# The high parts of the weight blocks by a converting DMA instead of a ScalarE cast

## The chip, the cores and the metric

One core of a Trainium2 chip runs the whole program. The metric is the device time of one execution in microseconds (us).

## The reference

The program is one step of a two-layer decoder trunk, D = 1024, on 1024 prompt tokens and 8 x 4 sample tokens that carry their own states. Cut to what the matmuls see:

```python
# layer 0, Hawk: W_LRU = 1536
xn = rmsnorm(x, g0)
xb, gate = split(xn @ a_w_in)            # 1024 -> 2 x 1536
h = rg_lru(causal_conv(xb))              # gates from 16 blocks of 96 x 96, then a scan over time
x = x + (h * silu(gate)) @ a_w_out       # 1536 -> 1024
# layer 1, HGRN2: 8 heads of 128
xn = rmsnorm(x, g1)
q, f, v, gate = split(xn @ b_w_in)       # 1024 -> 4 x 1024
o = gated_linear_recurrence(silu(q), f, v)
x = x + (rmsnorm(o) * silu(gate)) @ b_w_out
y = rmsnorm(x, final_gain)
```

The outputs are y and the new states, all in float32.

## The kernel before

Channels lie on the 128 partitions and tokens along the free axis. There are 1024 + 32 = 1056 columns, cut into three chunks of 352 (`CH`). The host has laid the weights out by output tile of 128 channels, so that one tile's weights are one 128 x 1024 matrix (an *item*): two blocks of 128 x 512, four K steps of 128 in each.

Products keep float32 accuracy with three matmuls in the shorter float32r type. A value x is held as a high part, x rounded to float32r, and a low part, x minus that. `mm3` (L239 to L243) multiplies high by high (L241), high weight by low activation (L242), low weight by high activation (L243). One item on one chunk is 8 K steps or 24 matmuls; on all three chunks it is 72.

The function `weights` (L371) prepares the blocks of one item. For each block SP issues a DMA of the float32 values from DRAM to a buffer `raw`; ScalarE (ACT) casts it to the high part (L383); then `subtract` (L313) gives the low part as raw minus high, on GpSimd (POOL) in the default case `e is G`, on VectorE (DVE) where the caller asks for it. `get` then hands out the K steps. The buffers go round in rings: three of `raw` (`wraw` in the profile), four of the high part (`whi`), four of the low part (`wlo`). With `at` the high and low parts go to places that the caller names, and the rings of high and low are left alone.

Those who call `weights`:

- `begin` (L862): the first six items of layer 0, in the first 60 us. Four of them split on DVE, and four have places of their own.
- `project0` (L414) and `by_chunk` (L421): the other input projections of layer 0, the gates and the convolution inputs.
- `out` (L634): output rows of layer 0, blocks of 128 x 384.
- `first1` (L715) and the dictionary `ahead` behind it: the first items of layer 1.
- the loop over `wo1` (L1629): output rows of layer 1, five K steps each, so a block of 512 and one of 128; the first two rows have places of their own.

Two other places prepare weights without it: `out_last` casts the last 384 K rows of layer 0's output weights by itself, and layer 1's head products (`seven`) use `low` (L315), where ACT writes minus the high part and POOL issues a DMA that adds the raw value to it in SBUF.

The order of the work is not written out by hand. Each operation of layer 0 goes into a list (class `Flow`) with its engine, an assumed duration, the keys that it reads and writes, and a priority. `plan` schedules the list on five queues (PE, DVE, ACT, POOL, SP) with a simple model of the DMA engines; `back` does the same from the end, to give each operation a latest start as its new priority; eight rounds of both are run, the best is kept, and `search` then tries 3000 random shifts of the operations planned in the first 60 us. The engines get their instructions in the resulting order. Layer 1 is a second list without the search. So a changed duration or engine of one kind of operation can move others anywhere in its layer.

PE runs this sequence of products in layer 0: the first six items chunk by chunk (`products`), gate(1), conv(1), gate(2), conv(2), out(0), gate(3) in part, conv(3), out(1), the rest of gate(3), `out_last`, `first1`. 48 filling matmuls of `ones` (L734) keep PE busy until data is there. Before `out_last`, `norm` and `scaled_parts` (L463) make the normalised activations that the next layer multiplies. In `first1` ACT takes a tanh of the product (L724) and POOL makes the two gate rows ST and a from it (L726), of which layer 1's first decay factors are made.

Of the kernel before, what the change touches and what calls it, by code (L numbers as in the profile page):

```python
# [209 lines left out]
def tile_trunk(ctx: ExitStack, tc: tile.TileContext, xT, prm, hc, w0, wg, wo0, w1, wo1, s_in,  # L210
               yT, h_out, c_out, sp_out, ss_out):
    nc = tc.nc
    V, S, G, T, Q = nc.vector, nc.scalar, nc.gpsimd, nc.tensor, nc.sync
# [82 lines left out]
    with ExitStack() as l0:  # L296
        pl = l0.enter_context(tc.tile_pool(name="l0", bufs=1, reuse_waits="tile"))
        fl = Flow("PE")

        def fixed(name, shape, dt=F32, pool=None):  # L300
            return (pool or pl).tile(shape, dt, tag=name, name=name)
# [7 lines left out]
        def dma(dst, src, r=(), w=(), prio=5, kb=180, q=Q):  # L309
            fl.add("SP" if q is Q else "ACT", 0.45, lambda: q.dma_start(dst, src), r, w, prio, kb * (1.0 if r else 0.75))  # L310
# [6 lines left out]
        def act(n, emit, r, w, prio=5, more=0.0):  # L317
            fl.add("ACT", 0.25 + 0.0007 * n + more, emit, r, w, prio)
# [7 lines left out]
        def subtract(e, n, b, x, a, r, w, prio):  # L326

            emit = lambda: e.tensor_tensor(b, x, a.bitcast(F32), op=ALU.subtract)  # L328
            if e is G:
                pool(n, emit, r, w, prio)  # L330
            else:
                dve(n, emit, r, w, prio, True)
# [38 lines left out]
        def weights(src, n, prio=2, e=G, at=None, q=Q, own=()):  # L371

            own = iter(own)
            got = []
            for a in range(0, n, 512):
                m = min(512, n - a)
                raw, *rk = next(own, None) or next(raws)
                if at:
                    (hi, hk), (lo, lk) = ((o[:, a:a + m], k) for o, k in at)
                else:  # L380
                    (hi, hk), (lo, lk) = next(his), next(los)
                dma(raw[:, :m], src[:, a:a + m], (), rk, prio, m / 2, q)
                act(m, lambda hi=hi, raw=raw, m=m: S.copy(hi[:, :m], raw[:, :m]), rk, (hk,), prio)  # L383
                subtract(e, m, lo[:, :m], raw[:, :m], hi[:, :m], (*rk, hk), (lk,), prio)
                got.append((hi, lo, hk, lk))

            def get(k):
                q = slice((k % 4) * 128, (k % 4 + 1) * 128)
                hi, lo, hk, lk = got[k // 4]
                return hi[:, q], lo[:, q], (hk, lk)  # L390

            return get
# [18 lines left out]
        def project0(items):  # L411

            for src, evac in items:
                w = weights(src, 1024)  # L414
                for c in range(NCH):
                    evac(c, *product(w, xcols(c)))
                    yield

        def by_chunk(items):

            ws = [weights(src, 1024) for src, _ in items]  # L421
            for c in range(NCH):
                for w, (_, evac) in zip(ws, items):
                    evac(c, *product(w, xcols(c)))
                    yield
# [204 lines left out]
        def out(g, src, dst):  # L630

            own = cycle([next(xos) for _ in range(NXO)] + [next(ts) for _ in range(3)] + [(x[:, :CH], k) for x, k in (next(xbs) for _ in range(3))])
            for m in range(KD):
                w = weights(wo0[m][:, 384 * g:384 * g + 384], 384)  # L634
                for c in range(NCH):
                    ps, pk = product(w, ycols(c))
                    x, xk = next(own)
                    dma(x, src[m][:, chunk(c)], ((g, m, c),), (xk,), 3)
                    dve(CH, lambda x=x, ps=ps: V.tensor_tensor(x, ps[:, :CH], x, op=ALU.add), (pk, xk), (xk,), 0)
                    dma(dst[m][:, chunk(c)], x, (xk,), ((g + 1, m, c),), 3)  # L640
                    yield
# [208 lines left out]
        raw = (halves[1][:8], [slots[i] for i in (1, 4, 7, 2, 5, 8)] + [halves[1][8], free[8]], free[:8])  # L850
# [82 lines left out]
    with ExitStack() as l1:  # L933
        p1 = l1.enter_context(tc.tile_pool(name="l1", bufs=1, reuse_waits="tile"))
        fl = Flow(side=0.4)
# [7 lines left out]
        at = fixed("attn", [128, 8, 128], F32, p1)  # L943
# [702 lines left out]
        for m in range(KD):  # L1646
            row = (xh, xl)[m // 4][4 + m % 4]
            hi, lo, hk, lk = row[:, :nl], row[:, nl:2 * nl], ("late", m, 0), ("late", m, 1)
            for k in (hk, lk):
                inherit(k, [("x", p, m % 4, x) for p in (2, 3) for x in range(2)])  # L1650
            raw, rk = next(raws)
# [60 lines left out]
        for a, n in OUT:  # L1712
# [4 lines left out]
            for m in range(KD):  # L1717
# [5 lines left out]
                hi, lo, wk = late[m]  # L1723
# [97 lines left out]
```

## Time and profile before

| | us |
|---|---|
| median of 2 runs | 1075.01 (1074.71 to 1075.32) |
| the profiled execution | 1074.84 |
| its span in the profile | 1073.1 |
| PE busy | 1050.9 |
| DVE busy | 745.6 |
| ACT busy | 663.7 |
| POOL busy | 504.5 |

The span runs from the first to the last recorded event; 1.74 us of the execution's time lie outside it. PE is TensorE's matmuls and PEld its weight loads, which overlap them; SP only issues DMAs. L383 is line 383 of the code. In a group of instructions stand line, engine, operation, output <- input, shape and count; behind the first bar the busy time and the mean duration in ns of one; behind the second the engine's idle time just before them and what ended most of it. A row of the timeline has start, duration, engine, line, operation and, in square brackets, the idle time before it with what ended it. A row on a releaser (`PE mm L242 <- POOL xl L328: 0.7, 1, 0.7`) has the total wait, how often, and the longest. Lines of DMA issues have the count, the size of one and the median time from issue to landing in us; the transfer lines that begin with q0 have packets, megabytes and the share of sixteen DMA engines over the span.

### The profile page before, as it was taken

The page shows a single profiled execution, that of the slowest core. Times are in us where ns is not written, and L with a number is a line of the kernel's source. Part 1 is how long each engine was busy: PE and PEld are TensorE (multiplying, and loading weights), DVE is VectorE, ACT ScalarE, POOL GpSimd, SP SyncE. Part 2 cuts the span into 40 slices and gives each one's busy share as a digit, 9 for nine tenths or more (in the row PEclk, how much of TensorE's full clock was granted, in tenths as well). Part 3 has the DMA queues.
Part 4 walks back from the last instruction along what each step waited for, and adds up shares of the span by engine and source line. Part 5 has one row for each costly group of instructions (what it writes and reads, how often), then busy time and mean ns, then how long its engine had stood idle before and what let it go on. Part 6 is the DMA issues. An engine that isn't in the chain of part 4 may idle for free.

```text
span 1073.1 us, 25672 instructions
## 1 busy us (share of the span) xinstructions
PE 1050.9 (98%) x10020; PEld 1023.3 (95%) x10020; DVE 745.6 (69%) x1481; ACT 663.7 (62%) x1493; POOL 504.5 (47%) x536
## 2 busy tenths in 40 slices
PE   9999999999999999999989999999999999999997
PEld 9999999999999999999989998989999999989996
DVE  7999996887987787274887556556565475674446
ACT  6578656867765964243467685858586767652323
POOL 3425353354543547455454454455455464541544
PEclk9999999999999999999989999999999999999999
DMA  9111112124832785373675564746465657555204
GB/s 302 60 28 43 56 48 72 58 60 127 270 104 67 217 258 168 108 242 121 188 200 110 130 140 100 178 93 156 89 151 112 155 112 169 140 161 166 84 1 162
DMA packets 92490, 139.59 MB, mean 130 GB/s; under 512 B 11344, under 2 KB 60496, under 8 KB 92368
## 3 DMA queue, kind: packets, MB, share of 16 engines
q1 hardware_dynamic: 75952, 109.49, 31.8%
q0 software_dynamic: 14112, 25.70, 14.3%
q10 hardware_dynamic: 2304, 2.77, 0.8%
q8 instruction: 78, 1.28, 0.5%
q14 instruction: 44, 0.36, 0.1%
HBM read 77.54 MB, written 29.81 MB: 100 GB/s over the span
## 4 chain that ended last, share of the span: by engine, by line
PE 86%; DVE 9%; DMA 3%; issue 1%; ACT 1%; POOL 0%; POOLq 0%; ACTq 0%; SPq 0%; DVEq 0%
PE mm L241 24%; PE mm L242 24%; PE mm L243 23%; PE hg L1057 2%; PE hg L1166 2%; DMA a<-xn 1%; PE hg L1274 1%; PE hg L572 1%; DVE R L1039 1%; PE hg L1276 1%; PE hg L241 1%; PE hg L242 1%; PE hg L243 1%; PE hg L1220 1%; DVE a L1240 1%
## 5 line engine op out<-in xcount | busy, mean ns | idle before, releaser
L241 PE MATMUL mm<-xh,whi 128*128 128x352 f32 (+1 forms) x1111 | 346.6, 312 | 5.7 <-DVE sg L1510 5.7
L242 PE MATMUL mm<-xl,whi 128*128 128x352 f32 (+1 forms) x1111 | 340.7, 307 | 0.0
L243 PE MATMUL mm<-xh,wlo 128*128 128x352 f32 (+1 forms) x1111 | 340.6, 307 | 0.0
L241 PEld LDWEIGHTS mm<-xh,whi 128*128 128x128 f32 x1111 | 209.0, 188 | 8.3 <-DVE sg L1510 6.8
L242 PEld LDWEIGHTS mm<-xl,whi 128*128 128x128 f32 x1111 | 209.3, 188 | 1.5
L243 PEld LDWEIGHTS mm<-xh,wlo 128*128 128x128 f32 x1111 | 209.1, 188 | 0.0
L328 POOL TENSOR_TENSOR wlo<-wraw,whi 128x512 fp32r<-128x512 f32 (+1 forms) x72 | 96.3, 1347 | 105.7 <-ACT whi L383 97.2
L241 PE MATMUL mm<-t,whi 128*128 128x264 f32 (+1 forms) x354 | 104.0, 294 | 0.0
L243 PE MATMUL mm<-t,wlo 128*128 128x264 f32 (+1 forms) x354 | 101.8, 288 | 2.0 <-DMA wlo<-wraw 2.0
L242 PE MATMUL mm<-t,whi 128*128 128x264 f32 (+1 forms) x354 | 101.9, 288 | 0.0
L504 DVE SCALAR_TENSOR_TENSOR k<-xb,prm_sb,k 128x352 f32<-128x352 f32 (+2 forms) x144 | 90.0, 636 | 11.0 <-ACT k L501 6.3
L315 POOL DMA_DIRECT2D wlo<-wraw x59 | 51.6, 888 | 65.6 <-ACT wlo L314 46.6
L1510 DVE TENSOR_TENSOR k<-mm,k 128x264 f32<-128x264 f32 x72 | 30.7, 430 | 62.2 <-PE mm L243 59.4
L243 PEld LDWEIGHTS mm<-t,wlo 128*128 128x128 f32 x354 | 67.2, 190 | 2.3 <-DMA wlo<-wraw 2.3
L241 PEld LDWEIGHTS mm<-t,whi 128*128 128x128 f32 x354 | 67.5, 191 | 0.5 <-ACT k L1487 0.2
L242 PEld LDWEIGHTS mm<-t,whi 128*128 128x128 f32 x354 | 67.5, 191 | 0.0
L587 POOL TENSOR_TENSOR k<-X 128x352 f32<-128x352 f32 x36 | 42.8, 1198 | 47.8 <-DVE R L588 38.6
L383 ACT CAST whi<-wraw 128x512 fp32r<-128x512 f32 (+2 forms) x75 | 41.3, 569 | 31.3 <-PE mm L242 19.8
L315 POOL DMA_DIRECT2D wlo<-R x36 | 33.5, 929 | 49.7 <-ACT wlo L314 48.2
L241 PE MATMUL mm<-yh,whi 128*128 128x352 f32 x153 | 49.9, 326 | 0.0
L243 PE MATMUL mm<-yh,wlo 128*128 128x352 f32 x153 | 49.4, 323 | 0.0
L242 PE MATMUL mm<-yl,whi 128*128 128x352 f32 x153 | 49.4, 323 | 0.0
(422 smaller groups left out, 2742.1 us busy)
## 6 DMA issues: line engine op xcount, KB each, us to landing
wraw<-in_w_dram SPq DMA_DIRECT2D x88, 256.0 KB, 3.1
wlo<-wraw POOLq DMA_DIRECT2D x59, 256.0 KB, 4.1
wlo<-R POOLq DMA_DIRECT2D x36, 256.0 KB, 4.0
wraw<-in_wo_dram SPq DMA_DIRECT2D x34, 192.0 KB, 2.5
si<-in_s_in_dram SPq DMA_DIRECT2D x8, 512.0 KB, 4.5
R<-in_w_dram SPq DMA_DIRECT2D x16, 256.0 KB, 3.8
out_ss_out_dram<-si SPq DMA_DIRECT2D x8, 512.0 KB, 2.6
sg<-x1b SPq DMA_DIRECT2D x21, 176.0 KB, 3.1
```

The costliest lines, as they stand in the source:

```text
L241: T.matmul(out, wh, xh, start=first, stop=False, skip_group_check=chained)
L242: T.matmul(out, wh, xl, start=False, stop=False, skip_group_check=chained)
L243: T.matmul(out, wl, xh, start=False, stop=last, skip_group_check=chained)
L315: fl.add("POOL", 0.93, lambda: G.dma_start(dst.bitcast(F32), src, accum_op=ALU.add), (*r, *w), w, prio, n / 2)
L328: emit = lambda: e.tensor_tensor(b, x, a.bitcast(F32), op=ALU.subtract)
L383: act(m, lambda hi=hi, raw=raw, m=m: S.copy(hi[:, :m], raw[:, :m]), rk, (hk,), prio)
L504: dve(u, lambda src=src, dst=dst, sh=sh, k=k: V.scalar_tensor_tensor(dst, sh(src, k), pc("cw", 12 * k + m), dst, op0=ALU.mult, op1=ALU.add ...
L572: fl.add("PE", 0.62, lambda ps=ps, i=i, c=c: T.matmul(ps[:96, :CH], gs[:, i, :], ST[:96, chunk(c)], start=True, stop=True), (("gs",), *((" ...
L587: pool(CH, lambda x=x, a=a, b=b: G.tensor_tensor(x, a.bitcast(F32), b.bitcast(F32), op=ALU.add), (ak, bk), (xk,), 3)
L1057: T.matmul(ps[32 * j:32 * j + 32, n * w:n * w + w], B[:, o:o + 32], q(slice(o, o + 32)), start=True, stop=True, tile_position=(0, 32 * j))
L1166: T.transpose(ps[:, n * 128:(n + 1) * 128], row[:, a:a + 128], ident)
L1510: dve(QT, lambda: V.tensor_tensor(o[0], z[0], u[0], op=ALU.add), (z[1], u[1]), (o[1],), 0)
```

## The change

Where `weights` splits on POOL and no places are named, the high part no longer comes from `raw`. POOL issues a second DMA of the same block from DRAM, into the float32r buffer, and the conversion is left to the DMA. The raw block is still loaded by SP, and the subtraction on POOL is as before; it now follows two transfers. The other blocks keep the cast.

```diff
@@ -380,7 +380,10 @@
                 else:
                     (hi, hk), (lo, lk) = next(his), next(los)
                 dma(raw[:, :m], src[:, a:a + m], (), rk, prio, m / 2, q)
-                act(m, lambda hi=hi, raw=raw, m=m: S.copy(hi[:, :m], raw[:, :m]), rk, (hk,), prio)
+                if e is G and at is None:
+                    fl.add("POOL", 0.95, lambda hi=hi, m=m, a=a: G.dma_start(hi[:, :m], src[:, a:a + m]), (), (hk,), prio, m / 2)
+                else:
+                    act(m, lambda hi=hi, raw=raw, m=m: S.copy(hi[:, :m], raw[:, :m]), rk, (hk,), prio)
                 subtract(e, m, lo[:, :m], raw[:, :m], hi[:, :m], (*rk, hk), (lk,), prio)
                 got.append((hi, lo, hk, lk))
```

72 blocks take the new way: 44 of 128 x 512 of the input projections (36 in layer 0, 8 in layer 1), 16 of 128 x 384 in `out`, and 12 of the layer-1 output rows (six of 512, six of 128). Three casts stay. Lines behind L382 are three higher in the changed kernel; the new DMA is L384.

Layer 1's order is nearly the same but for the replaced instructions. Layer 0 is planned anew. Three places of it follow; `x3` behind a row means three such in a row.

PE, start of the program. `hg<-ones` are the filling matmuls, `whi` and `wlo` the parts of the first item's weights, `xh` and `xl` those of the activations. Before:

```order
L734 MATMUL hg<-ones 128x128 x29
L241 MATMUL mm<-xh,whi 128x352
L242 MATMUL mm<-xl,whi 128x352
L243 MATMUL mm<-xh,wlo 128x352
L241 MATMUL mm<-xh,whi 128x352
L242 MATMUL mm<-xl,whi 128x352
L243 MATMUL mm<-xh,wlo 128x352
L734 MATMUL hg<-ones 128x128 x9
L241 MATMUL mm<-xh,whi 128x352
L242 MATMUL mm<-xl,whi 128x352
L243 MATMUL mm<-xh,wlo 128x352
L734 MATMUL hg<-ones 128x128 x2
```

In the changed kernel the same stretch of PE reads:

```order
L737 MATMUL hg<-ones 128x128 x39
L241 MATMUL mm<-xh,whi 128x352
L242 MATMUL mm<-xl,whi 128x352
L243 MATMUL mm<-xh,wlo 128x352
L737 MATMUL hg<-ones 128x128 x9
L241 MATMUL mm<-xh,whi 128x352
L242 MATMUL mm<-xl,whi 128x352
L243 MATMUL mm<-xh,wlo 128x352
```

The filling matmuls stood between the first products in six pieces (the last three lie behind the rows shown) and now stand in two.

DVE, in the last column chunk of `out_last`. L703 (now L706) adds a product to the residual `sg`; L453 and L456 (now L456 and L459) write the inverse norms of the second chunk into a diagonal matrix `xb` for the matmul that broadcasts them; L463 (now L466) scales that chunk's rows, `xo` and `sg`; L328 is the low part of a scaled row. Before:

```order
L453 TENSOR_TENSOR xb_133<-ident,nr_130 128x256
L456 TENSOR_SCALAR xb_133<-ident,nr_130 128x96
L328 TENSOR_TENSOR xl<-sg,xh 128x352
L703 TENSOR_TENSOR sg<-mm,sg 128x352 x3
L328 TENSOR_TENSOR xl<-sg,xh 128x352
L463 SCALAR_TENSOR_TENSOR xo_135<-xo_135,prm_sb,hg 128x352
L463 SCALAR_TENSOR_TENSOR xo_136<-xo_136,prm_sb,hg 128x352
L463 SCALAR_TENSOR_TENSOR sg<-sg,prm_sb,hg 128x352
L703 TENSOR_TENSOR sg<-mm,sg 128x352
```

In the changed kernel:

```order
L706 TENSOR_TENSOR sg<-mm,sg 128x352
L456 TENSOR_TENSOR xb_133<-ident,nr_130 128x256
L459 TENSOR_SCALAR xb_133<-ident,nr_130 128x96
L706 TENSOR_TENSOR sg<-mm,sg 128x352 x7
L466 SCALAR_TENSOR_TENSOR xo_135<-xo_135,prm_sb,hg 128x352
L466 SCALAR_TENSOR_TENSOR sg<-sg,prm_sb,hg 128x352
L466 SCALAR_TENSOR_TENSOR xo_136<-xo_136,prm_sb,hg 128x352
L328 TENSOR_TENSOR xl<-xo_135,xh 128x352
```

The scaling of the second chunk stood among the last chunk's evictions and now stands behind the last of them.

POOL, at the change of layers. L726 (now L729) makes the gate rows ST and a from the tanh `k` of `first1`; the `wlo` rows are the low parts of the items in `ahead`; L1050 (now L1053) is layer 1's first instruction. Before:

```order
L726 TENSOR_SCALAR ST<-k,smalls 128x352
L726 TENSOR_SCALAR a<-k,smalls 128x352
L328 TENSOR_TENSOR wlo<-wraw,whi 128x512 x3
L726 TENSOR_SCALAR ST<-k,smalls 128x352
L726 TENSOR_SCALAR a<-k,smalls 128x352
L328 TENSOR_TENSOR wlo<-wraw,whi 128x512
L1050 COPY gp<-sg 128x8
```

In the changed kernel:

```order
L729 TENSOR_SCALAR ST<-k,smalls 128x352
L384 DMA whi<-in_w_dram 128x512
L729 TENSOR_SCALAR a<-k,smalls 128x352
L384 DMA whi<-in_w_dram 128x512 x2
L328 TENSOR_TENSOR wlo<-wraw,whi 128x512
L384 DMA whi<-in_w_dram 128x512
L328 TENSOR_TENSOR wlo<-wraw,whi 128x512
L729 TENSOR_SCALAR ST<-k,smalls 128x352
L729 TENSOR_SCALAR a<-k,smalls 128x352
L328 TENSOR_TENSOR wlo<-wraw,whi 128x512 x2
L1053 COPY gp<-sg 128x8
```

Four issues have come in ahead of the last pair of gate rows, and one subtraction has moved from ahead of that pair to behind it.

## The prediction

> **What bounds the kernel now.** I read the page first: the busy shares of the engines, then the chain that ended last.
>
> ```profile
> span 1073.1 us, 25672 instructions
> ...
> PE 1050.9 (98%) x10020; PEld 1023.3 (95%) x10020; DVE 745.6 (69%) x1481; ACT 663.7 (62%) x1493; POOL 504.5 (47%) x536
> ...
> PE 86%; DVE 9%; DMA 3%; issue 1%; ACT 1%; POOL 0%; POOLq 0%; ACTq 0%; SPq 0%; DVEq 0%
> ```
>
> PE is busy for all but 22.2 us of the span, and ACT, whose work the change takes away, carries 1% of the chain. The stage table says where PE waits. Its columns are PE, PEld, DVE, ACT and POOL busy with instruction counts, then granted clock, DMA share and GB/s.
>
> ```profile
> 0.00:60.00 60.00, 57.82 (x376) 56.52 (x377) 53.56 (x132) 35.55 (x75) 21.00 (x33) 1.00 0.50 162
> 60.00:500.00 440.00, 440.00 (x2710) 433.54 (x2709) 345.10 (x598) 283.05 (x553) 205.07 (x228) 1.00 0.39 120
> 250.00:300.00 50.00, 50.00 (x303) 48.54 (x302) 40.15 (x67) 37.85 (x68) 22.97 (x23) 1.00 0.72 225
> 350.00:400.00 50.00, 50.00 (x306) 48.79 (x305) 41.64 (x65) 40.43 (x70) 25.20 (x19) 1.00 0.80 251
> 470.00:480.00 10.00, 10.00 (x63) 9.79 (x62) 9.30 (x19) 5.76 (x12) 6.21 (x7) 1.00 0.98 336
> 540.00:545.00 5.00, 2.96 (x21) 2.75 (x20) 5.00 (x7) 3.77 (x7) 1.87 (x3) 0.92 1.04 178
> 545.00:550.00 5.00, 5.00 (x34) 5.00 (x33) 1.96 (x5) 2.35 (x6) 0.40 (x1) 0.74 1.04 286
> ```
>
> From 60 to 500 us, where 52 of the 72 changed blocks are used, PE does not stop: 440 us for 2710 matmuls, 0.162 us each. Nothing can be won there; the change can only uncover a wait. PE does wait around 540 us, at the change of layers, and the clock falls to 0.74 behind that gap.
>
> **The change, part by part.** The prices come from these groups and transfers.
>
> ```profile
> L328 POOL TENSOR_TENSOR wlo<-wraw,whi 128x512 fp32r<-128x512 f32 (+1 forms) x72 | 96.3, 1347 | 105.7 <-ACT whi L383 97.2
> L315 POOL DMA_DIRECT2D wlo<-wraw x59 | 51.6, 888 | 65.6 <-ACT wlo L314 46.6
> L383 ACT CAST whi<-wraw 128x512 fp32r<-128x512 f32 (+2 forms) x75 | 41.3, 569 | 31.3 <-PE mm L242 19.8
> q0 software_dynamic: 14112, 25.70, 14.3%
> wraw<-in_w_dram SPq DMA_DIRECT2D x88, 256.0 KB, 3.1
> wlo<-wraw POOLq DMA_DIRECT2D x59, 256.0 KB, 4.1
> wlo<-kt POOLq DMA_DIRECT2D x3, 256.0 KB, 5.3
> ```
>
> *Removed:* 72 of the 75 casts, 72 x 0.569 = 41 us of ACT. They lie beside PE's work; on the path they are worth 0.
>
> *Added on POOL:* 72 DMA issues. No casting DMA is in the trace. The nearest row is the accumulating DMA that POOL issues already, 0.89 us: 64 us of POOL. From 60 to 500 us that is 52 x 0.89 = 46 us on top of 205 of 440 us, so POOL has the room, and the cover is PE's queue of prepared blocks.
>
> *Added latency:* the high part is no longer a cast of 0.57 us but a transfer. Bounds are 3.1 us (SP's plain load of the same block) and 5.3 us (the slowest POOL row); I take 4.1 us, the POOL row with the most cases. In steady state an item is 72 matmuls, 72 x 0.162 = 11.7 us, and its two buffers come back one whole item before they are due. Landing 4.1, two subtractions of 1.35 and two hops of 0.2 make 7.2 us, which fits with 4.5 us to spare. Output blocks have one buffer of four each, so three items of 27 x 0.162 = 4.4 us pass before one is due: 4.1 + 1.35 + 0.4 fits in 13.1. Cost 0.
>
> *Added traffic:* q0 spends 14.3% of 1073.1 us on 98 transfers of 256 KB, 1.57 us of all 16 engines each. Added are 50 of 1.57, 16 of 1.18 and 6 of 0.39, about 100 us. In the two output stages the DMA engines have 36 and 40 us of work in 50 us; eight 384-column blocks (9.4 us) and up to four of 512 (6.3 us) bring this to 52 and 56. So up to 2 + 6 = 8 us could come out; but part of it is work for the next stage, and at 470 us PE ran on at a DMA share of 0.98. I take 0 and keep 8 for the range.
>
> *Start of the program.* The planner also orders the first 60 us anew. Of the 48 filling matmuls 39 now stand ahead of the first product, where there were 29, and 9 behind its first three matmuls.
>
> ```profile
> 1.04 8.57 PE L734 MATMUL hg<-ones 128*128 128x128 f32 x58 [1.04 <-DVE ones L253]
> 10.41 2.17 PE L734 MATMUL hg<-ones 128*128 128x128 f32 x18
> 16.49 0.41 PE L241 MATMUL mm<-xh,whi 128*128 128x352 f32 x1
> ```
>
> The trace shows two passes each, so 39 take 78 x 0.148 = 11.5 us and the first product starts at 12.6 us; with the 9 others (2.2 us) the stream starts at 15.3. At 16.5 us PE has then done about 3.5 groups of three matmuls where it had done 6: 1.2 us behind. But PE waited 2.2 us in the first 60 us, and data that came later than PE can make that up. Between -1 and +1.2, I take 0.
>
> *Last output product.* The scaling of the second column chunk, which `first1` needs, has moved behind that product's last eviction (second order view), since its broadcast matmul now stands there. Before, it stood at 471 us:
>
> ```profile
> 471.36 0.75 PE L458 MATMUL hg<-xb,ones 128*128 128x352 f32 x2
> 485.47 0.33 PE L241 MATMUL mm<-xh,whi 128*128 128x352 f32 x1
> ```
>
> Now it comes at 485.5, so eight scalings of 0.5 us and six subtractions of 0.5 end near 493; PE wants the last at 485.5 + 0.4 + 3.9 + 3.4 = 493. About 0.4 us, between 0 and 1.5.
>
> *Change of layers.* Here POOL's queue matters: four issues and two subtractions now stand ahead of the last gate row ST, on which the chain runs. The old casts show when each buffer came free.
>
> ```profile
> 504.01 0.62 ACT L383 CAST whi<-wraw 128x512 fp32r<-128x512 f32 x1 [0.85 <-PE mm L242]
> 505.92 0.62 ACT L383 CAST whi<-wraw 128x512 fp32r<-128x512 f32 x1 [1.29 <-PE mm L242]
> 507.83 0.62 ACT L383 CAST whi<-wraw 128x512 fp32r<-128x512 f32 x1 [0.93 <-PE mm L242]
> 509.96 0.46 ACT L724 ACTIVATE k<-mm 128x352 f32<-128x352 f32 x1 [1.51 <-PE mm L243]
> ...
> 510.53 0.65 POOL ST L726
> 511.20 1.31 DVE R L1069
> ```
>
> The last two lines are from the chain of waits: ST is on it. The third issue ends at 508.7; the first transfer has landed at 508.1, so its subtraction runs 508.7 to 510.0; the fourth issue (its buffer is free by 509.9) to 510.9; the second subtraction to 512.2; then ST, 1.7 us late. Behind it wait the decay scalings on DVE and PE with them. A landing of 5.3 us makes it 2.3; if the rest of the chain absorbs some, 0.5.
>
> *Tail.* The output weights of layer 1 use two buffers a row.
>
> ```profile
> 940.94 0.61 ACT L383 CAST whi<-wraw 128x512 fp32r<-128x512 f32 x1
> 942.17 0.28 ACT L383 CAST whi<-wraw 128x128 fp32r<-128x128 f32 x1
> ...
> 944.81 1.08 POOL L328 TENSOR_TENSOR xl<-k,xh 128x352 fp32r<-128x352 f32 x1 [1.19 <-ACT xh L1594]
> ```
> ```profile
> PE mm L242 <- POOL xl L328: 0.7, 1, 0.7
> ```
> ```profile
> 985.66 0.82 ACT L383 CAST whi<-wraw 128x512 fp32r<-128x512 f32 x2 [2.88 <-PE mm L242]
> 995.68 0.82 ACT L383 CAST whi<-wraw 128x512 fp32r<-128x512 f32 x2 [1.94 <-PE mm L242]
> 1002.91 0.82 ACT L383 CAST whi<-wraw 128x512 fp32r<-128x512 f32 x2 [1.81 <-PE mm L242]
> ```
>
> At 941 us the subtraction of the second block now waits for its landing, with the split xl behind it, for which PE waits already. If the issue comes as late as the cast did, it lands at 945.0 and xl starts at 946.5, 1.7 us late (2.9 at 5.3); if it comes when POOL is idle, nothing is lost. I take 0.9. Later, buffers come back 7.2 to 10.0 us before they are due and a refill takes 4.1 + 1.35 + 0.4 = 5.9: nothing.
>
> The Trainium skill (DMA: Bandwidth & Descriptors, section "Anatomy of one DMA") fits a POOL-issued transfer by 2.0 us plus its bytes over 436 bytes per ns, an estimate of 2.6 us here. The row says 4.1, and even SP's plain load 3.1, so the trace disagrees; by the page the tail's 0.9 would go and the sum be 1076.9.
>
> **Sum.** 0 + 0 + 0.4 + 1.7 + 0.9 = 3.0 us on the profiled execution's 1074.84 (span 1073.1 and 1.74 around it): 1077.8 us, and on the median of the runs, 1075.01, hardly more. The ends of the terms give -0.5 and +16: 1074.3 to 1091.
>
> **The rivals.**
>
> *Landing becomes the bound (slower).* If a casting transfer takes much longer than an accumulating one, the buffers' round trip decides: in layer 0 above 11.7 - 3.1 = 8.6 us of landing. At 10 us, 18 items lose 1.4 each (25 us) and three rows of the tail 1.7, 2.9 and 4.6 (9 us): 1112. For it: the DMA share is 0.8 before the change. Against: no POOL row is above 5.3. Chance 12%.
>
> *The new order gains.* ACT's 41 us or the new start could fill the idle time before 60 us, at most 60 - 57.82 = 2.2 us: 1072.6. Against it: ACT's 1% of the chain. Chance 8%.
>
> *Issues held up by DVE.* A POOL issue might stand still while a DVE instruction runs, 745.6 us / 1481 = 0.5 us a time: 2 us more ahead of ST and 1 in the tail, 1080.8. Against it: DVE is busy 69% of the time, and the mean issue of 888 ns leaves little for it. Chance 5%. The Trainium skill (SBUF — State Buffer, "Who interferes with whom") has this rule: descriptors that GpSimd writes are locked out while VectorE runs in a two-port mode; this row shows no such hold.
>
> *All of PE's idle time goes (faster by 2%).* That needs 21.5 of its 22.2 us: 1053. Chance 2%.
>
> That the casts stay in place is excluded: the order of the changed kernel has 72 DMAs on POOL and 72 casts fewer on ACT. If the transfer did not round, the time would be the same.
>
> **How the numbers follow.** My own case has 73%, at 1077.8 us. The range is 1072.5 to 1097: down to the gain, up over the bounds of the terms to a landing of about 9.2 us, where the slow rival passes 2%. Under 2% a measurement of this kernel can hardly be told from no change. Faster by over 2% is 2%; slower is the landing rival's 12%; 86% is left within.
>
> **What would show it.** PE's idle time between 60 and 500 us stays near 0; POOL grows by about 64 us and ACT falls by 41; the casting transfer lands in about 4 us; ST is 1 to 2 us later against the end of `first1`. I am wrong if PE waits for wlo in layer 0, if the output stages stretch, or if the issue takes well over 0.9 us.

## The result, and the profile after

The changed kernel takes 1087.43 us (two runs, 1086.51 to 1088.36) against 1075.01: 1.0115 times before, 95% interval 1.0072 to 1.0159. That is slower, by 12.4 us, within the 2% that the forecast gave most of its chance and inside its range (1072.5 to 1097), but four times the 2.8 us that it had worked out. The profiled execution took 1086.51 us, 11.7 more than that of before.

From the page of the changed kernel: span, engines, chain.

```profile
span 1084.7 us, 25729 instructions
...
PE 1058.2 (98%) x10020; PEld 1028.8 (95%) x10020; DVE 740.4 (68%) x1481; ACT 629.9 (58%) x1421; POOL 535.6 (49%) x608
...
PE 83%; DVE 9%; issue 3%; DMA 2%; POOL 2%; ACT 1%; POOLq 0%; ACTq 0%; DVEq 0%; SPq 0%
```

ACT has lost 33.8 us and POOL gained 31.1. POOL has come from 0 to 2% of the chain; PE is idle for 26.5 us of the span (1084.7 - 1058.2) instead of 22.2, 4.3 us more of the 11.6, so most of the loss isn't seen as idle time. The groups that answer to the old cast, and the landings:

```profile
L328 POOL TENSOR_TENSOR wlo<-wraw,whi 128x512 fp32r<-128x512 f32 (+1 forms) x72 | 90.6, 1267 | 45.3 <-DMA whi<-in_w_dram 15.2 <-PE mm L243 11.3 <-DMA whi<-in_wo_dram 8.8
L384 POOL DMA_DIRECT2D whi<-in_w_dram x44 | 25.1, 571 | 36.7 <-PE mm L243 21.0 <-PE mm L242 10.7 <-PE hg L243 3.7
L384 POOL DMA_DIRECT2D whi<-in_wo_dram x28 | 15.9, 568 | 27.2 <-PE mm L242 14.6 <-PE mm L243 5.6 <-PE hg L243 5.4
```
```profile
q0 software_dynamic: 24480, 42.35, 20.1%
...
whi<-in_w_dram POOLq DMA_DIRECT2D x44, 256.0 KB, 3.3
```

An issue costs POOL 0.57 us, 41 us for all, and a block lands 3.3 us after it. Traffic of q0 went from 14.3% of 1073.1 us to 20.1% of 1084.7: 65 us more. Each of these is below what the forecast took (0.89, 4.1, 100). The price of the operation itself is not where the time went.

All 6024 matmuls of `mm3` stand on PE in both kernels in nearly the same order, so the n-th of one can be held against the n-th of the other. Two rows show how; they are the 97th matmul, before and then after:

```profile
32.06 0.42 PE L241 MATMUL mm<-xh,yh 128*128 128x352 f32 x1 [1.01 <-DVE sg L532]
```
```profile
34.96 0.43 PE L241 MATMUL mm<-xh,yh 128*128 128x352 f32 x1 [3.15 <-DVE sg L535]
```

34.96 - 32.06 = 2.9 us behind at that place. The same at nine places, worked out in this way from the traces, for all kernels of this study (us behind before's trace; the heading is the time in before; "end" is the last such matmul):

| kernel | 67 | 429 | 437 | 485 | 515 | 571 | 773 | 929 | end |
|---|---|---|---|---|---|---|---|---|---|
| changed | 2.5 | 4.6 | 6.4 | 6.1 | 9.2 | 10.5 | 7.5 | 7.2 | 10.7 |
| wo1_only | -0.2 | -0.2 | -0.2 | -0.2 | -0.2 | -2.6 | -6.4 | -6.5 | -6.0 |
| l0_only | 4.0 | 6.5 | 8.4 | 8.1 | 12.2 | 13.1 | 8.5 | 9.0 | 8.4 |
| old_plan | -0.1 | 32.9 | 32.9 | 42.5 | 48.8 | 52.4 | 47.2 | 47.8 | 54.7 |
| one_load | 4.3 | 6.3 | 7.8 | 7.5 | 10.8 | 13.5 | 8.4 | 8.2 | 7.3 |
| start_old | 0.4 | 0.0 | 3.5 | 3.4 | 6.5 | 5.9 | 2.5 | 2.4 | 4.6 |
| cast_new_order | 4.3 | 7.3 | 7.3 | 7.0 | 8.1 | 9.1 | 5.9 | 6.3 | 6.7 |
| w1_cast | 5.8 | 7.8 | 7.8 | 7.5 | 8.6 | 11.4 | 5.6 | 5.9 | 6.4 |
| wo0_cast | 5.2 | 7.2 | 7.2 | 6.9 | 11.1 | 14.1 | 7.0 | 8.7 | 11.7 |
| before_seed2 | 1.9 | 3.8 | 3.8 | 3.8 | 4.0 | 3.6 | 0.8 | 1.5 | 1.6 |
| after_seed2 | 5.4 | 6.4 | 8.6 | 8.3 | 11.4 | 9.8 | 5.2 | 7.2 | 9.1 |
| start_w1 | 0.4 | 0.0 | 0.3 | 0.0 | 0.8 | 2.7 | -1.0 | 0.6 | 1.0 |
| steady | 0.8 | 0.4 | 0.6 | 0.4 | 1.2 | -2.1 | -6.0 | -5.2 | -5.9 |

So the changed kernel loses 2.5 us in the start, 2.1 from there to 429 us, 1.7 at the first blocks of the last output product (429 to 437), 3.1 in that product's end and the change of layers (485 to 515), and 3.5 in the tail (929 to the end); some 3 us are taken back at 571 to 773 us, where before waits for 2.2 and 1.8 us (at 651 and 710 us) and the changed kernel, coming later, for 1.7 (at 719). After the last matmul 0.9 more go. wo1_only, whose layer 0 has before's orders, is within 0.2 us of it at all five places up to 515 us; behind that, single executions of the same orders differ by several us (the runs of before went from 1067.6 to 1079.3 in one set), so the columns from 571 on carry less.

A part of the differences between the rows is the clock. In the traces' clock records the granted clock is 1.0 or 0.5, and, but for the last stretch of each trace, it is 0.5 for 3.4 us or a multiple. Six kernels have the changed kernel's order of the first 60 us: changed, l0_only, one_load, cast_new_order, w1_cast and wo0_cast. In all six PE waits about 3 us at 35 us. The stage behind it in the changed kernel, in cast_new_order and in w1_cast (PE, PEld, DVE, ACT, POOL busy with counts, clock, DMA share, GB/s):

```profile
34.00:44.00 10.00, 9.04 (x57) 8.83 (x58) 10.00 (x24) 5.94 (x13) 3.88 (x4) 1.00 0.40 128
```
```profile
34.00:44.00 10.00, 8.71 (x45) 8.50 (x46) 8.90 (x21) 5.85 (x12) 3.85 (x4) 0.83 0.44 135
```
```profile
34.00:44.00 10.00, 8.36 (x35) 7.86 (x35) 8.19 (x18) 5.36 (x11) 4.21 (x5) 0.66 0.48 145
```

The clock stays up in the changed kernel (2.5 us behind at 67), is halved for 3.4 us in l0_only, one_load and cast_new_order (4.0 to 4.3) and for 6.8 us in w1_cast and wo0_cast (5.2 to 5.8). So this one order costs some 2.5 us by itself, and up to 3.3 more with the clock.

*The start.* PE's 97th matmul waits 3.15 us for a gate product. DVE's rows ahead of it, before and then after:

```profile
29.98 1.14 DVE L438 TENSOR_TENSOR R<-R,xo 128x352 f32<-128x352 f32 x2
31.05 0.52 DVE L532 TENSOR_TENSOR sg<-mm,R 128x352 f32<-128x352 f32 x1
```
```profile
31.17 2.86 DVE L441 TENSOR_TENSOR R<-R,xo 128x352 f32<-128x352 f32 x3
33.96 0.94 DVE L535 TENSOR_TENSOR sg<-mm,R 128x352 f32<-128x352 f32 x2
```

DVE waits for nothing ahead of either; the new order puts one more sum of squares (R) ahead of the gate's first eviction, and the three take 2.86 us. They don't take it evenly: the first two last 0.5 us each, the third 1.62, beside a subtraction on POOL that starts with it.

```profile
32.41 1.62 DVE L441 TENSOR_TENSOR R<-R,xo 128x352 f32<-128x352 f32 x1
```
```profile
32.37 1.28 POOL L328 TENSOR_TENSOR yl<-wraw,yh 128x512 fp32r<-128x512 f32 x1
```

In both traces such a sum takes 0.50 to 0.53 us where no long two-input instruction of POOL overlaps it, and up to 1.4 (before) or 1.6 us (changed) where one does. So the order also decides what DVE's work runs beside.

*429 to 437.* The last weight block of `out_last`, which is still cast by ACT, is late: its float32 values land so that ACT casts at 439.35, POOL subtracts at 440.04, and PE, in the rows below, waits for both.

```profile
439.35 0.62 ACT L666 CAST whi<-wraw 128x512 fp32r<-128x512 f32 x1 [1.68 <-DMA wraw<-in_wo_dram]
```
```profile
440.02 0.43 PE L241 MATMUL mm<-yh,whi 128*128 128x352 f32 x1 [0.34 <-ACT whi L666]
...
441.36 0.43 PE L243 MATMUL mm<-yh,wlo 128*128 128x352 f32 x1 [0.76 <-POOL wlo L667]
```

*Change of layers.* POOL's queue, with the four issues and four subtractions, then PE's first product of layer 1:

```profile
511.36 0.64 POOL L384 DMA_DIRECT2D whi<-in_w_dram  x1 [0.88 <-PE mm L242]
512.05 0.64 POOL L729 TENSOR_SCALAR a<-k,smalls 128x352 f32<-128x352 f32 x1
513.30 0.56 POOL L384 DMA_DIRECT2D whi<-in_w_dram  x1 [0.61 <-PE mm L243]
515.24 0.53 POOL L384 DMA_DIRECT2D whi<-in_w_dram  x1 [1.38 <-PE mm L242]
515.78 1.30 POOL L328 TENSOR_TENSOR wlo<-wraw,whi 128x512 fp32r<-128x512 f32 x1
517.20 0.57 POOL L384 DMA_DIRECT2D whi<-in_w_dram  x1
518.12 1.28 POOL L328 TENSOR_TENSOR wlo<-wraw,whi 128x512 fp32r<-128x512 f32 x1 [0.36 <-DMA whi<-in_w_dram]
519.39 0.63 POOL L729 TENSOR_SCALAR ST<-k,smalls 128x352 f32<-128x352 f32 x1
520.02 0.63 POOL L729 TENSOR_SCALAR a<-k,smalls 128x352 f32<-128x352 f32 x1
520.87 3.72 POOL L328 TENSOR_TENSOR wlo<-wraw,whi 128x512 fp32r<-128x512 f32 x2 [0.22 <-DMA whi<-in_w_dram]
```
```profile
522.93 0.43 PE L243 MATMUL mm<-xh,wlo 128*128 128x352 f32 x1 [1.24 <-POOL wlo L328]
```

Three of the four issues wait for a matmul to give a buffer back; ST starts at 519.39 instead of 510.53, 8.9 us later, of which PE was already 7.0 behind at 506 us. And the third subtraction stands behind ST and a, so PE waits 1.24 us for the weights themselves: it is 7.7 us behind just ahead of that wait and 9.2 just after it.

*Tail.* POOL, then PE:

```profile
950.94 0.54 POOL L384 DMA_DIRECT2D whi<-in_wo_dram  x1 [1.74 <-PE mm L243]
952.51 1.76 POOL L328 TENSOR_TENSOR wlo<-wraw,whi 128x512 fp32r<-128x512 f32 x1 [1.03 <-DMA whi<-in_wo_dram]
954.24 1.11 POOL L328 TENSOR_TENSOR xl<-k,xh 128x352 fp32r<-128x352 f32 x1
```
```profile
955.40 0.66 PE L242 MATMUL mm<-xl,t 128*128 128x352 f32 x1 [1.46 <-POOL xl L328]
```

The subtraction waits for a landing, xl waits behind it, and PE's wait for xl has grown from 0.7 to 1.5 us. Part of the 3.5 us here is the clock: it is halved for 6.8 us from 954.8 us, in before for 3.4 us from 947.0.

### The profile page after: what moved, and what is told of

Same layout as the page of the kernel before. It is cut to its first block, busy times and chain, and to the rows that moved or that the text cites. A ratio compares the mean times of both kernels' runs of the same rounds, so it can differ in the third digit from the quotient of the medians.

```text
span 1084.7 us, 25729 instructions
## 1 busy us (share of the span) xinstructions
PE 1058.2 (98%) x10020; PEld 1028.8 (95%) x10020; DVE 740.4 (68%) x1481; ACT 629.9 (58%) x1421; POOL 535.6 (49%) x608
## 3 DMA queue, kind: packets, MB, share of 16 engines
q0 software_dynamic: 24480, 42.35, 20.1%
## 4 chain that ended last, share of the span: by engine, by line
PE 83%; DVE 9%; issue 3%; DMA 2%; POOL 2%; ACT 1%; POOLq 0%; ACTq 0%; DVEq 0%; SPq 0%
PE mm L241 23%; PE mm L242 23%; PE mm L243 23%; PE hg L1060 2%; PE hg L1169 1%; PE hg L1277 1%; PE hg L575 1%; PE hg L1279 1%; DVE R L1042 1%; PE hg L241 1%; PE hg L243 1%; PE hg L242 1%; DMA a<-xn 1%; PE hg L1223 1%; DVE t L328 1%
## 5 line engine op out<-in xcount | busy, mean ns | idle before, releaser
L328 POOL TENSOR_TENSOR wlo<-wraw,whi 128x512 fp32r<-128x512 f32 (+1 forms) x72 | 90.6, 1267 | 45.3 <-DMA whi<-in_w_dram 15.2
L571 ACT ACTIVATE R<-hg,smalls 128x352 f32<-128x352 f32 x72 | 38.3, 551 | 15.3 <-DVE R L611 7.6
```

The source lines that it names most:

```text
L571: act(CH, lambda ps=ps, R=R, i=i, j=j, hb=hb, m=m: S.activation(R[:, i, j], ps[:, :CH], AF.Tanh, bias=hb[:, m:m + 1], scale=0.5), (pk, ("s ...
```

## The experiments

The ratios are to before on the same chip, with 95% intervals. In all but the first two sections the operations keep a chosen order, so that one thing is changed at a time.

**wo1_only and l0_only: the change in two halves.** `fl.until` is set in layer 0's list alone.

```diff
-                if e is G and at is None:
+                if e is G and at is None and fl.until is None:    # wo1_only; l0_only: ... and fl.until
```

> Only the 12 blocks of layer 1's output rows are loaded by the converting DMA; layer 0 keeps before's orders on every engine. In the changed kernel PE's lag behind before grew from 7.3 us at 919 us to 10.5 at 951 us. Theory 'late blocks' (a block is ready later, and places without reserve lose it): this happens here too, +2.5 to +3.3 us, 1077.5 to 1078.3. Rival 'new plan' (the loss comes from layer 0 being ordered anew, the tail only passes it on): 1075.0, +0.3 at most. Layer 0 is also a control: if the 0.8 ns by which each matmul was longer between 60 and 434 us came from the added transfers, it is 160.0 ns here as before; if it is scatter between runs, it can be anything from 159 to 161.

> The complement: the 60 blocks of layer 0's list are loaded by the converting DMA, those of layer 1's output rows are cast. Late blocks and new plan alike: the changed kernel without its tail, 1087.4 less 2.5 to 3.3, so 1084.1 to 1084.9. If the two parts are not additive (the tail has reserve that the late layer 0 uses up), 1087.

wo1_only: 1.0005 (0.9985 to 1.0026); l0_only: 1.0089 (1.0065 to 1.0113), 1083.73 us. The 12 blocks of the tail alone cost nothing that shows in the time, against the 2.5 us and more that 'late blocks' expected: a miss, the rival was right, and PE is only 0.5 us further behind at the end than at 929 us. The wait of the tail is there all the same, as long as in the changed kernel:

```profile
939.71 0.43 PE L242 MATMUL mm<-xl,t 128*128 128x352 f32 x1 [1.46 <-POOL xl L328]
```

Layer 0's 60 blocks cost 9.7 us, about as expected. wo1_only also shows that the slower matmuls between 67 and 429 us are not scatter: with before's orders their time is before's.

**old_plan: the converting DMA at the cast's place.**

```diff
-                    fl.add("POOL", 0.95, lambda hi=hi, m=m, a=a: G.dma_start(hi[:, :m], src[:, a:a + m]), (), (hk,), prio, m / 2)
+                    act(m, lambda hi=hi, m=m, a=a: G.dma_start(hi[:, :m], src[:, a:a + m]), rk, (hk,), prio)
```

> All 72 blocks are loaded by the converting DMA, but the planner is told the cast's engine and price, and the issue is put out at the planned place of the cast: PE, DVE and SP have before's orders word for word. Late blocks: first items, steady state as before (reserve 4 us and more); about 3 us lost at the change of layers and 3 in the tail, and 0 to 3 at the first blocks of the last output product: 1079 to 1084. New plan: its first 60 us are before's, so 2.5 us are back there and the rest with them, 1075 to 1077. If PE waits for blocks everywhere because the issue now comes as late as the cast did, more than 1090.

1.0525 (1.0489 to 1.0560), 1129.84 us: the last of the three cases. The stages from 60 us, in old_plan and then in the changed kernel (PE, PEld, DVE, ACT, POOL busy with counts, clock, DMA share, GB/s):

```profile
60.00:430.00 370.00, 349.56 (x2069) 337.08 (x2068) 276.91 (x483) 216.18 (x415) 173.70 (x220) 0.98 0.46 132
```
```profile
60.00:430.00 370.00, 370.00 (x2258) 363.74 (x2257) 305.20 (x525) 232.62 (x446) 188.50 (x239) 1.00 0.50 146
430.00:480.00 50.00, 48.91 (x305) 47.98 (x304) 17.46 (x40) 14.20 (x31) 27.34 (x30) 1.00 0.49 150
```

POOL is no busier and the DMA share no higher, yet PE idles for 20 us. POOL's subtractions in old_plan say how (the changed kernel's group stands above, with 45.3 us of idle time ahead of it):

```profile
L328 POOL TENSOR_TENSOR wlo<-wraw,whi 128x512 fp32r<-128x512 f32 (+1 forms) x72 | 89.6, 1248 | 160.1 <-issue 51.6 <-PE mm L243 40.0 <-DMA whi<-in_wo_dram 19.7
```

Whatever the row names as the releaser, 61 of the 65 waits, 158 us of them, end within 0.14 us of the landing of a converting block. An issue that comes as late as the cast did is followed in POOL's queue by the subtraction that waits for its landing, and other POOL work stands behind both. So the latency is hidden only where the plan issues ahead of time: that part of the new order is what the change needs. The new order of the first 60 us is not; start_old and steady below do without it.

**one_load: the change without its traffic.** The float32 load of the 72 blocks keeps its place in the plan and is not sent; the low part is high minus high, so this kernel leaves the low parts of these weights out.

```diff
-                dma(raw[:, :m], src[:, a:a + m], (), rk, prio, m / 2, q)
+                if e is G and at is None:
+                    fl.add("SP", 0.45, lambda: None, (), rk, prio, m / 2 * 0.75)
+                else:
+                    dma(raw[:, :m], src[:, a:a + m], (), rk, prio, m / 2, q)
...
-                subtract(e, m, lo[:, :m], raw[:, :m], hi[:, :m], (*rk, hk), (lk,), prio)
+                low_from = hi.bitcast(F32) if e is G and at is None else raw
+                subtract(e, m, lo[:, :m], low_from[:, :m], hi[:, :m], (*rk, hk), (lk,), prio)
```

> The changed kernel with its orders, but the 72 blocks' float32 values are not loaded: the low part is made as high minus high, so the low parts of these weights are left out. The converting DMA is then the only load, and the traffic is before's. Late blocks: the landing, issue and subtraction stay, 1085 to 1087. Rival 'traffic' (the doubled loads slow all others down, above all in the two output stages): the 1.8 us at the first blocks of the last output product and what follows go, and the 2 us between 60 and 434 us, 1079 to 1083.

1.0083 (1.0057 to 1.0108), 1083.99 us: between the two expectations. Its first stage:

```profile
60.00:430.00 370.00, 370.00 (x2259) 363.96 (x2258) 299.52 (x533) 232.69 (x446) 176.81 (x240) 1.00 0.40 113
```

The DMA share is 0.40 instead of 0.50, and PE has done 2259 matmuls instead of 2258. Up to 571 us it loses at the same places by nearly the same amounts as l0_only; only in the tail, where the changed kernel lost 3.5, it loses nothing. In layer 0 traffic is not the cause; in the tail it may be a part, but there the clock differs too.

**start_old and cast_new_order: the order alone.** For these and what follows, each cast keeps the converting DMA as its alternative, so that a plan can be made with the one and the order filled with the other.

```diff
+    def swap(self, which):
+        for i, (what, op) in self.alt.items():
+            if what in which:
+                self.ops[i], self.alt[i] = op, (what, self.ops[i])
...
# start_old
+        old = self.solve(tries, first)
+        self.swap(ALL)
+        best = self.solve(tries, first)
+        if first:
+            key = [o if o < first else max(n, first) for o, n in zip(old[1], best[1])]
+            best = self.plan(key)
# cast_new_order
+        self.swap(ALL)
+        best = self.solve(tries, first)
+        self.swap(ALL)
+        self.links()
+        best = self.plan(best[1])
```

> The changed kernel, all 72 blocks by the converting DMA, but the operations that before planned in its first 60 us keep before's order; the rest follows the changed order. No converting DMA is used by PE in these 60 us. Theory 'new order' for the start: the 2.5 us (4.0 and 4.3 us in the two other runs with this start) by which PE is behind before at 67 us go to 0 +- 0.3, and the whole comes to 0.7 to 0.9% over before instead of 1.2%. Rival 'late blocks' (the first converted blocks are what the start waits for): 2.5 us remain. Beside it: if the 0.8 ns more per matmul between 60 and 434 us come from the order of the start, they go too (159.5 instead of 160.9 ns).

> Before's casts on ScalarE, none of the 72 converting DMAs, but the operations have the starts of the changed kernel's plan as their priorities, so the first 60 us are word for word the changed kernel's and the rest is close to it. New order for the start: 2.5 to 4.3 us behind before at 67 us. Late blocks for the rest: nothing is lost at 434 us, at the change of layers or in the tail, so 0.2 to 0.5% over before. If order is the whole cause: 0.8 to 1.2% over before.

start_old: 1.0058 (1.0036 to 1.0081), 1079.38 us. cast_new_order: 1.0082 (1.0056 to 1.0109), 1082.76 us, more than the 0.2 to 0.5% expected of it and at the lower end of what was put for order as the whole cause. It has no converting DMA at all: the order alone costs 0.8%, where the whole change costs 1.15%. In the table: with before's order in the first 60 us PE is 0.4 us behind at 67 us, and with the new order, converted blocks or not, 2.5 to 5.8, the clock included. And the start decides more than itself. The stage from 60 to 430 us in start_old, then in cast_new_order:

```profile
60.00:430.00 370.00, 370.00 (x2272) 364.19 (x2271) 304.78 (x526) 233.21 (x447) 192.23 (x242) 1.00 0.51 147
```
```profile
60.00:430.00 370.00, 369.80 (x2252) 362.91 (x2251) 302.80 (x533) 256.70 (x499) 172.26 (x187) 1.00 0.37 110
```

Without idle time PE does 2272 matmuls (0.1629 us each in the mean) after the old start, and 2258 (0.1639) after the new one in the changed kernel; before had the same stage with 2273:

```profile
60.00:430.00 370.00, 370.00 (x2273) 364.18 (x2272) 310.12 (x526) 259.41 (x504) 172.67 (x194) 1.00 0.37 115
```

That is the 2.1 us between 67 and 429, 0.6% of a stage that looks full in every profile. It goes with the order of the first 60 us: not with the casts, and not with the traffic. It isn't even over the stage: from 67 to 90 us nothing is lost, and between 110 and 180 us, in start_old against the changed kernel, most matmuls differ by 3 ns or less and a quarter take 5 to 13 ns longer. Why, these runs don't show. start_old's 3.5 us from 429 to 437 hold, beside the late block, a stretch of 3.4 us at half clock.

**w1_cast and wo0_cast: one kind of block cast again, in the changed order.**

```diff
+        self.swap(ALL)
+        best = self.solve(tries, first)
+        self.swap({"in_w1_dram"})      # wo0_cast: {"in_wo0_dram"}
+        self.links()
+        best = self.plan(best[1])
```

> The changed kernel and its order, but the 8 blocks of layer 1's first items are cast on ScalarE again, at the places of their DMA issues. Late blocks: of the 3.2 to 4.4 us that PE loses between 485 and 530 us in the runs with the converting DMA at least 2 come back, since there POOL's issues, the landing and then the subtraction stand between the buffer's release and the matmul: 0.8 to 0.9% over before. Rival: the place loses as much, because it is the activations' scaling, which the new order has moved behind the last eviction, that comes late there: 1.2%.

> The changed kernel and its order, but the 16 blocks of the two output stages of layer 0 are cast again. Of the 1.5 to 1.9 us lost at 434 to 442 us, where the first blocks of the last output product come late: if the converting DMAs of the output stages hold up POOL and the buffers of float32 values there, they go; if the doubled traffic of the stage before does it, they go as well, but the kernel without the float32 loads had still lost 1.5 us; if it is the order, they stay. Time 1.0% over before or less in the first case, 1.2% in the other.

w1_cast: 1.0075 (1.0046 to 1.0105); wo0_cast: 1.0114 (1.0082 to 1.0146). With the eight blocks of layer 1's first items cast, 485 to 515 us cost 1.1 us instead of 3.1 (4.1 in l0_only, 4.2 in wo0_cast): 2 to 3 us are theirs, as expected. The 1.1 that stay come with the order, since cast_new_order has them too: the scaling behind the last eviction and, for 0.3, the second of the two broadcast matmuls, which now stands behind the 485 mark. The loss at 429 to 437 goes in both kernels, and in cast_new_order; so no one kind of block makes it. The last block of `out_last` has little reserve left in the new order: its cast starts 8.1 us ahead of the matmul that uses it in before, about 2.0 in cast_new_order, w1_cast and wo0_cast, and 0.7, with PE waiting, in the changed kernel. Either set of issues used it up.

**before_seed2 and after_seed2: another lot.**

```diff
-        rng = Random(1)
+        rng = Random(2)
```

> Before, nothing converted, only with another seed for the 3000 random shifts that the planner tries in the first 60 us. Its fillers stand 44 and 4, much as the changed kernel's (39 and 9). Theory 'lot' for the start: the 2.5 to 5.8 us that the changed order loses there are the luck of one search, which an equally good plan for the same work can lose as well: PE 2 to 6 us behind before at 67 us, 160.9 ns a matmul after it instead of 159.9, and 0.4 to 0.8% over before. Rival 'price': the planner pays for issues and landings and so finds a worse start; then another seed without them costs under 1 us, 1.000 +- 0.2%.

> The changed kernel with the other seed; fillers in pieces of 34, 10 and 2, more like before's. Lot: the start differs from the changed kernel's by 2 us or more in one direction, and the rest loses as before (1.5 to 3.5 us at 429 to 437 us, 3 us at 485 to 515, 1 to 3 in the tail): 0.5 to 1.3% over before. Price: 2.5 to 5.8 us lost at 67 us again, 1.0 to 1.2% over before.

before_seed2: 1.0018 (0.9991 to 1.0046); after_seed2: 1.0101 (1.0070 to 1.0132). Before, with nothing converted, loses 1.9 us in the start and 1.9 more to 429 us only because its search drew other numbers; its stage counts 2261 matmuls:

```profile
60.00:430.00 370.00, 370.00 (x2261) 364.18 (x2260) 314.09 (x535) 258.89 (x503) 170.96 (x190) 1.00 0.37 113
```

The clock stays up in that start. That is the lot, and the rival (that paying for issues makes the start worse) is not needed for it. But the lot's weight in the whole time came out lower than expected: most of the 3.8 us are taken back by 773 us in this execution, and the interval holds 1. The changed kernel's other lot is 5.4 us behind at 67, but its clock is halved for 6.8 us there, and the first lot's order was 5.2 and 5.8 behind in the two traces where it met the same; so no difference between the two starts is shown. It loses 1.0 instead of 2.1 from there to 429, and then about as much at 429 to 437 (2.2) and 485 to 515 (3.1) as the first.

**start_w1 and steady: what remains.** As start_old, with the eight blocks of layer 1's first items cast (start_w1), and the 12 of layer 1's output rows too (steady).

```diff
         best = self.solve(tries, first)
+        self.swap({"in_w1_dram"})      # steady: {"in_w1_dram", "in_wo1_dram"}
+        self.links()
+        key = best[1]
         if first:
             key = [o if o < first else max(n, first) for o, n in zip(old[1], best[1])]
-            best = self.plan(key)
+        best = self.plan(key)
```

> The changed kernel with before's order in the first 60 us and the 8 blocks of layer 1's first items cast: 64 blocks remain with the converting DMA. With before's start 0.0 us were lost at 429 us, and with these 8 cast nothing at 429 to 437 us and 1.1 us instead of 3.1 at 485 to 515. So 1 us behind at 515 us and 1 to 3 us more in the tail: 0.1 to 0.35% over before. If start and first items don't add up: 0.5%.

> As the kernel just before it, and the 12 blocks of layer 1's output rows cast too: the 52 blocks of layer 0 between 60 and 480 us are left with the converting DMA. Theory 'late blocks': these are the blocks with 4 us and more of reserve, so they cost nothing: PE 0 +- 0.3 us behind before at 429 us, 1 us at 515, 0.0 to 0.2% over before. If they cost by their traffic or by POOL's time after all, more than 0.3%.

start_w1: 1.0012 (0.9991 to 1.0032), 1075.27 us; steady: 0.9983 (0.9962 to 1.0005), 1072.14 us. Steady's two stages:

```profile
60.00:430.00 370.00, 370.00 (x2272) 364.18 (x2271) 303.16 (x526) 233.59 (x448) 191.07 (x241) 1.00 0.49 147
430.00:480.00 50.00, 50.00 (x313) 49.51 (x313) 18.81 (x40) 15.52 (x32) 27.73 (x28) 1.00 0.52 166
```

52 of the 72 blocks cost nothing: PE does not stop. Nor do they gain anything that can be told from 0: steady's interval holds 1, and its profiled execution has the clock halved only in its last 5 us, where before's has it halved for 3.4 us three times earlier as well. No version here clearly beats before.

## Why the prediction was right in its class and four times too small

*Right: the steady state.* "Cost 0" for the 52 blocks of layer 0, and "Nothing can be won there", stand in steady's rows. "The change can only uncover a wait" does not: in the changed kernel 2.1 us went there with PE busy throughout. What the forecast did not say is that this needs the issue ahead of the cast's place: it argued from buffers ("an item ... come back one whole item before they are due") and left out that in POOL's one queue the waiting subtraction holds up all behind it. old_plan is that case, 55 us.

*Right: the last product.* PE lost 0.9 us from 485 to 506, 0.3 of it the moved broadcast, so about 0.6 where 0.4 was forecast (bound 1.5).

*Right in size, by another path: the change of layers.* ST was to come 1.7 us late, and came 1.9 late, by the queue of issues and subtractions that was named; w1_cast takes most of the loss away. PE lost 2.2 us from 506 to 515 (forecast 1.7, bound 2.3). But the forecast put this down to ST and "the decay scalings on DVE and PE with them", and PE lost it before the work that waits for ST: 0.4 at the second subtraction, where its matmul starts at 519.45 just after that ends at 519.40, and 1.5 at the third. These are PE's own waits for low parts of the weights, and the sum had no term for them. That the size came out is luck. What ST's lateness cost behind that isn't settled: at the next long wait, for an accumulating DMA at 554 us, the changed kernel stands 2.99 us where before stood 2.04, but of the other kernels with the new order after 60 us those with these eight blocks converted wait 1.6 to 2.6 us there, and those with them cast up to 2.3.

Its sign "I am wrong if PE waits for wlo in layer 0" was met: by 0.76 us at 441 us and 1.24 at 523. POOL grew by 31 us instead of 64, since an issue takes 0.57 us, and ACT fell by 34 instead of 41.

*Half right: the tail.* xl came later behind a subtraction that waits for a landing, as put. The wait for xl grew by 0.7 us, in wo1_only too, near the 0.9 forecast. PE lost 3.5 there in this trace, but over all kernels that is not a steady price: wo1_only had 0.5 there and start_w1 0.4. 1.7 us of the 3.5 are a pause between two matmuls for which no releaser shows:

```profile
944.65 0.42 PE L1231 MATMUL mm<-si,ab 128*32 128x128 f32 x7 [1.67 <-issue]
```

What it waits for stays open. The longer stretch at half clock is in the 3.5 too. The sum of the tail is between 0 and 3 us (start_w1 less steady is 0.3%, with intervals that overlap).

*Wrong: the start.* The step that failed is "Between -1 and +1.2, I take 0". It compared PE's queue alone: first product at 12.6 us (measured 12.1), stream from 15.3 (measured 14.6), and then trusted that "data that came later than PE can make that up". The data came later by DVE's order, which was not looked at: PE's 3.15 us wait at 35 us is for DVE, which had one sum more ahead of the eviction and one that took three times as long. With the slower matmuls that follow it, the start cost 4.6 us, the largest term; start_old gives back 0.6% of 1.15%.

*Wrong: the output stages.* "I take 0 and keep 8", for traffic. 1.7 us were lost just there, at the stage's end, but one_load loses 1.5 of it with the traffic gone, and w1_cast and wo0_cast lose none with it there. It was reserve, taken by order and POOL's issues.

So for the two seams that it named the sum was somewhat low (0.9 + 2.2 for 2.1 forecast); 4.6 of the start and 1.7 of the last product's first blocks were missing, and the tail lost more in this trace than its term. The 12% for a landing that bounds, as it was put, did not come: 3.3 us is far below 8.6.

The range held by its upper bounds, above all the 8 us for traffic, which were for other causes: that it holds the result is luck. The 5% for issues held up by DVE did not come either: all 72 issues took between 0.53 and 0.76 us. The Trainium skill (DMA: Bandwidth & Descriptors, section "Anatomy of one DMA") gave the estimate of 2.6 us for this transfer; the converting one took 3.3 in the median, so page and row of before (4.1) erred by 0.7 and 0.8 to either side.

## What to carry to other kernels

A converting DMA is cheap to issue (0.57 us) and lands in 3.3 us for 256 KB, so it can take the place of a cast wherever a block is due some item later, if the issue is moved ahead of the consumer in its queue; at the places with no reserve, the seams between stages, it is dearer than the cast. Where a planner with a random search sets the order, every change draws a new lot: hold the old order and exchange the one operation, or draw several lots of both, before a difference of half a per cent is put down to the change. And of a reordered start, hold the order of the engine that feeds the bounding one against the old order too, here DVE's, and what runs beside it.

## What the runs showed of the hardware that was not expected

The same instructions on a PE that never idles took 0.1629 or 0.1639 us each in the mean over 370 us, by the order of work that had ended before (rows above: 2272 and 2273 against 2258, 2259 and 2261). After the old order it repeats to one matmul (before, start_old, steady), after the new one too (changed, one_load); its cause is open.

A sum of squares on DVE that takes 0.5 us alone took up to 1.6 us beside a POOL subtraction (rows of 32.4 us above).

At the change to layer 1's second product, PE waits for an accumulating DMA, in before for 2.04 us and in wo1_only, whose orders are the same up to there, for 1.23:

```profile
543.83 0.39 PE L243 MATMUL mm<-t,wlo 128*128 128x264 f32 x1 [2.04 <-DMA wlo<-wraw]
```
```profile
542.70 0.39 PE L243 MATMUL mm<-t,wlo 128*128 128x264 f32 x1 [1.23 <-DMA wlo<-wraw]
```

Behind the longer wait the granted clock was 0.74 for 545 to 550 us; behind the shorter one it stayed at 1.00:

```profile
545.00:550.00 5.00, 5.00 (x160) 4.82 (x159) 2.56 (x7) 2.68 (x8) 0.86 (x1) 1.00 1.05 302
```

The Trainium skill (TensorE: Matmul & The Clock Gate, section "Why this matters for your kernels") warns of idle gaps of about 3 us and more. Here a gap of 2.0 us was followed by the lower clock, and the 3.15 us at 35 us of the changed kernel by none, where the same wait in w1_cast (3.17 us) went with 6.8 us of it. So the length of the gap alone did not decide it here. Such dips are one reason why single runs of one kernel lie up to 12 us apart (over the 29 runs of before in one set, the lower the mean granted clock, the longer the time, correlation -0.5), and why stages behind them should be compared over many runs.
